# The output projection of an encoder layer as seven block products

## The chip, the cores and the metric

One core of a Trainium2 chip runs the kernel. The metric is device time in microseconds for one execution; three timed runs are shown, beside one execution taken by the hardware profiler.

## The reference

One encoder layer works on two independent groups ("prompt" and "sample") with shared weights. A group is a matrix x of 1024 tokens by 1024 channels. An input projection feeds four kinds of heads (retention, HGRN2, mLSTM, SSD); their outputs, 512 channels each, are concatenated to `mixed`, 1024 tokens by 2048 channels. What matters here is what comes after:

```python
y = jnp.einsum('bte,ed->btd', mixed, w_out)          # w_out: 2048 x 1024
x = _layer_norm(DN_ALPHA * x + y, ln_g, ln_b)
gate = jax.nn.sigmoid(jnp.einsum('btd,de->bte', x, w_ple_gate).astype(jnp.float32))
return (x + gate * jnp.einsum('btp,pd->btd', p, w_ple_proj)).astype(x.dtype)
```

`p` has 256 channels. All arrays are float32.

## The kernel before

**Numbers in two parts.** A projection operand in float32 is split in a high and a low part of the type float32r (`split`: ScalarE copies to the high part, VectorE subtracts to get the low one). A product a·b is then three matmuls: high·high, high·low, low·high. A full-width matmul has a stationary operand of 128x128 and a moving one of 128x512.

**Order of the work.** For each group 14 head units run one after another (`ORDER`); each writes its 128 channels of `mixed`, channel-major, to DRAM (`mix_d`). After both groups' units comes the tail, which the change rewrites: four blocks (group, half of the tokens). Tile pools with rotating buffers order the work: `pt` (PB = 10 buffers of 1032 columns), `rt` (RB = 7), `ht` (HB = 12 of 512 columns), weight tiles `wh`/`wl` (WB = 3 pairs of 1024 columns), staging tiles `ws` (SB = 4). Projection accumulators take the four banks of `psj`, everything else the four of `pss`. A static scheduler fixes each engine's instruction order by priority, which is program order, shifted by `late`; weight splits are moved 600 places ahead (`EARLY`). All transfers shown here go through the one queue of SyncE (SP), in that order.

**A block.** `op_half` (L1090) computes 512 output columns for 512 tokens: 16 contraction tiles, for each four token tiles of three matmuls, into the four banks. `stream` (L318) brings the weights in. The split parts of `mixed` for one block lie in 32 tiles of their own (`x_tile`, L302); during the second `op_half` of a block, `load_mix` (L315) replaces them tile by tile with those of the next block. At the end each bank is added to the scaled residual input (L160). `layer_norm` (L1111) normalises the four token tiles (the root is a power on GpSimd), transposes them on TensorE and splits them again. `gate` (L1130) makes the 1024 gated output channels of 512 tokens: per 128 channels 24 matmuls for the gate, 6 for the projection of p, then ScalarE, VectorE and the store.

**Order of the blocks.** The gate of a block is held back (`pend`) and runs between the two `op_half` of the next block, so that the layer norm has matmuls beside it. At the last block the held gate comes after the second `op_half`, then the block's own layer norm, then its own gate:

```python
op_half(g, hf, 1, ys, None if last else blocks[n + 1])
xn = parts(last)
if last and pend:
    gate(*pend)
layer_norm(ys, xn)
pend = (g, hf, xn)
```

## Time and profile before

| what | us |
|---|---|
| timed runs, median of 3 | 2713.09 |
| timed runs, lowest and highest | 2709.48, 2713.47 |
| span of the profiled execution, first to last instruction | 2708.0 |
| of that, the tail (from 2106 us on) | 602.0 |

The profiled execution has no separate timing beside its span; the median of the timed runs stands 5.1 us above it. Engines are named PE (TensorE matmuls), PEld (weight loads into TensorE), DVE (VectorE), ACT (ScalarE), POOL (GpSimd) and SP (SyncE, here the issuer of DMAs). L174 is the line of the kernel that issues every split matmul, L148 and L151 are ScalarE's copy and VectorE's two-input operation, whoever calls them. `po` are the banks of the output projection, `pg` and `pq` those of the gate, `ptl` those of the transposes. A matmul's own duration overlaps its neighbours'; pace is read from starts in the chain of waits.

### The profile page before, as it was taken

The numbers are of one execution on the slowest core, as the hardware profiler recorded it, in microseconds if no ns is written. First come the engines' busy times: TensorE is split into PE (matmuls) and PEld (weight loads), VectorE is DVE, ScalarE is ACT, GpSimd is POOL, SyncE is SP. The second block draws the span as 40 slices with busy tenths as digits, with TensorE's granted clock in tenths as the row PEclk, the third lists the DMA queues.
The fourth block names the chain that finished last, engine by engine and source line by source line (L and its number), as shares of the span: only waits on it lengthen the run. The fifth ranks groups of instructions, "written<-read, shape, count | busy, mean of one in ns | idle before, by whom it ended". The sixth has DMA issues, their size and how long they took to land.

```text
span 2708.0 us, 43819 instructions
## 1 busy us (share of the span) xinstructions
PE 2665.3 (98%) x16874; PEld 2384.2 (88%) x16874; DVE 1806.3 (67%) x4417; ACT 1095.3 (40%) x2197; POOL 55.6 (2%) x48
## 2 busy tenths in 40 slices
PE   9999999999999999999999999999999999999999
PEld 8889988879899999999898888989999888888887
DVE  7778768878755555787786878855455555546455
ACT  6656523444422313655533444432222343333323
POOL 0000000000000000000000000000000000000000
PEclk9999999999999999999999999999999999999999
DMA  4111011334321213111111241432122434535333
GB/s 148 47 41 39 24 51 41 94 94 94 86 71 48 78 40 105 44 48 35 41 38 41 75 105 51 91 105 67 56 63 89 164 121 136 190 122 195 128 113 105
DMA packets 172945, 225.15 MB, mean 83 GB/s; under 512 B 13888, under 2 KB 82112, under 8 KB 172736
## 3 DMA queue, kind: packets, MB, share of 16 engines
q1 hardware_dynamic: 172736, 222.34, 27.0%
q8 instruction: 133, 2.18, 0.3%
q14 instruction: 76, 0.62, 0.1%
HBM read 196.86 MB, written 25.43 MB: 82 GB/s over the span
## 4 chain that ended last, share of the span: by engine, by line
PE 93%; DVE 3%; DMA 2%; ACT 1%; issue 1%; POOL 0%; SPq 0%; DVEq 0%; ACTq 0%; POOLq 0%
PE pj L174 53%; PE po L174 13%; PE pg L174 7%; PE pov L177 5%; PE psc L177 5%; PE pst L177 4%; PE ptr L399 3%; PE pin L177 2%; PE pq L174 2%; DMA ub<-ud 1%; DMA ub<-fd 1%; DVE x L160 0%; DMA ws<-in_wp 0%; PE ptl L1125 0%; ACT wh L148 0%
## 5 line engine op out<-in xcount | busy, mean ns | idle before, releaser
L174 PE MATMUL pj<-wl,xh 128*128 128x256 f32 (+1 forms) x2304 | 664.2, 288 | 0.0
L174 PE MATMUL pj<-wh,xh 128*128 128x256 f32 (+1 forms) x2304 | 663.6, 288 | 0.3
L174 PE MATMUL pj<-wh,xl 128*128 128x256 f32 (+1 forms) x2304 | 662.7, 288 | 0.0
L151 DVE TENSOR_TENSOR wl<-ws,wh 128x512 fp32r<-128x512 f32 (+1 forms) x488 | 313.8, 679 | 303.0 <-ACT wh L148 299.8
L148 ACT ACTIVATE wh<-ws 128x512 fp32r<-128x512 f32 (+1 forms) x488 | 280.7, 617 | 468.3 <-PE pj L174 234.4
L174 PEld LDWEIGHTS pj<-wh,xh 128*128 128x128 f32 x2304 | 441.4, 192 | 2.6 <-DVE hB L154 1.1
L174 PEld LDWEIGHTS pj<-wl,xh 128*128 128x128 f32 x2304 | 441.6, 192 | 1.4
L174 PEld LDWEIGHTS pj<-wh,xl 128*128 128x128 f32 x2304 | 441.6, 192 | 0.6
L174 PE MATMUL pj<-xh,wh 128*128 128x512 f32 x1024 | 415.9, 406 | 5.8 <-ACT wh L148 5.8
L174 PE MATMUL pj<-xh,wl 128*128 128x512 f32 x1024 | 414.7, 405 | 0.0
L174 PE MATMUL pj<-xl,wh 128*128 128x512 f32 x1024 | 413.3, 404 | 0.0
L174 PEld LDWEIGHTS pj<-xh,wh 128*128 128x128 f32 x1024 | 194.2, 190 | 40.6 <-ACT wh L148 5.8
L174 PEld LDWEIGHTS pj<-xl,wh 128*128 128x128 f32 x1024 | 194.3, 190 | 34.7
L174 PEld LDWEIGHTS pj<-xh,wl 128*128 128x128 f32 x1024 | 194.1, 190 | 34.7 <-DVE wl L151 0.2
L174 PE MATMUL po<-wl,xh 128*128 128x512 f32 x512 | 202.9, 396 | 0.0
L174 PE MATMUL po<-wh,xh 128*128 128x512 f32 x512 | 202.1, 395 | 0.0
L174 PE MATMUL po<-wh,xl 128*128 128x512 f32 x512 | 202.1, 395 | 0.0
L174 PE MATMUL pg<-xn,wh 128*128 128x512 f32 x384 | 120.2, 394 | 0.0
L174 PEld LDWEIGHTS po<-wl,xh 128*128 128x128 f32 x512 | 96.2, 188 | 21.0
L174 PEld LDWEIGHTS po<-wh,xl 128*128 128x128 f32 x512 | 96.2, 188 | 20.4
L174 PEld LDWEIGHTS po<-wh,xh 128*128 128x128 f32 x512 | 96.2, 188 | 20.0 <-DVE g L157 0.2
L151 DVE TENSOR_TENSOR xl<-xr,xh 128x512 fp32r<-128x512 f32 x96 | 63.9, 690 | 68.5 <-ACT xh L148 66.5
(285 smaller groups left out, 4262.6 us busy)
## 6 DMA issues: line engine op xcount, KB each, us to landing
ws<-in_wp SPq DMA_DIRECT2D x472, 256.0 KB, 3.3
mix<-hZ SPq DMA_DIRECT2D x64, 256.0 KB, 2.8
ub<-fd SPq DMA_DIRECT2D x64, 256.0 KB, 7.3
ub<-ud SPq DMA_DIRECT2D x64, 256.0 KB, 7.1
xr<-mix SPq DMA_DIRECT2D x64, 256.0 KB, 5.1
xr<-in_xT SPq DMA_DIRECT2D x32, 256.0 KB, 5.1
xr<-in_x SPq DMA_DIRECT2D x32, 256.0 KB, 5.0
out<-sg SPq DMA_DIRECT2D x32, 256.0 KB, 2.0
```

Of the source, the lines that this page charges most:

```text
L148: S.activation(o, i, AF.Copy, scale=scale)
L151: V.tensor_tensor(o, a, b, op)
L174: TE.matmul(o, l, r, start=start, stop=stop)
L177: TE.matmul(o, l, r, start=start, stop=stop)
L399: TE.transpose(o[0:s.shape[1], P * n:P * n + s.shape[0]], s, ident[0:s.shape[0], 0:s.shape[0]])
```

## The change

The tail no longer works by halves of the tokens. For a group, `mixed` (tokens in 2 halves, channels in 2 halves) times `w_out` (channels in 2 halves, columns in 2 halves) is a product of 2x2 blocks, and is computed with seven block products instead of eight, in Winograd's form of Strassen's method. Each product has 512 tokens, 1024 channels (8 contraction tiles) and 512 columns, and takes the four `psj` banks. `PROD` lists them in order with their operands: `("p", ...)` is a block as it is, `("c", ...)` a sum that is kept in a running tile (`RUN`), `("s", ...)` a sum used once. Four products need sums of blocks of `mixed`, and four sums of blocks of `w_out`; both kinds work on 128x512 tiles, the first on GpSimd, the second on VectorE (`fetch`). `join` puts a finished product into the output blocks, adding the residual when a block is to be complete. `prep_x` prepares the operands of the product after next (or, at m = 5, of the next group's first), into the two sets of 16 tiles that the halves had before. The first half of the tokens is normalised after the product numbered 3, and transposed between the matmuls of the last two products. Then come both gates of the group; the second half is transposed between the matmuls of the first gate. The pools grow: PB 10 to 12, RB 7 to 8, SB 4 to 5; the scratch for dynamic DMAs is set to 1024 bytes.

The diff, without the comments and docstrings that it also removes:

```diff
-PB, RB, HB, WB, SB, SSB = 10, 7, 12, 3, 4, 3
+PB, RB, HB, WB, SB, SSB = 12, 8, 12, 3, 5, 3
+SCRATCH = 1024
 SLACK = [0, 0]
 EARLY = 600
-L = [160, 500, 80, 100, 180, 80, 180]
...
-        def load_mix(g, hf, n):
-            x_tile(n // NKT, n % NKT, mix_d[g][n, :, 512 * hf:512 * hf + 512])
-
...
-        # ======================= output projection, layer norm, per-layer input gate =======================
-        def op_half(g, hf, n, ys, nxt=None):
-            """512 columns of the residual sum of 512 tokens."""
+        ADD, SUB = ALU.add, ALU.subtract
+        X11, X12, X21, X22 = [("p", i, j) for i in range(2) for j in range(2)]
+        RUN = ("k",)
+        PROD = [
+            (1, X11, X11),
+            (2, X12, X21),
+            (5, ("c", X21, X22, ADD), ("c", X12, X11, SUB)),
+            (6, ("c", RUN, X11, SUB), ("c", X22, RUN, SUB)),
+            (3, ("s", X12, RUN, SUB), X22),
+            (7, ("s", X11, X21, SUB), ("s", X22, X12, SUB)),
+            (4, X22, ("s", RUN, X21, SUB)),
+        ]
+        KH = DI // P // 2
+        run = {}
+        def mix_at(g, a, k):
+            return mix_d[g][KH * a[2] + k, :, 512 * a[1]:512 * a[1] + 512]
+        def out_at(b, k):
+            off, n, kt = PIECE_AT[("out", b[2])]
+            src = wp[off:off + P * kt * n].rearrange("(p f) -> p f", p=P)
+            r = KH * b[1] + k
+            return src[:, r * n:r * n + n]
+        def fetch(new, at, spec, k, key):
+            add = nc.gpsimd.tensor_tensor if key[0] == "x" else tt
+            def get(a, o=None):
+                if a == RUN:
+                    return run[key][k]
+                o = new() if o is None else o
+                nc.sync.dma_start(o, at(a, k))
+                return o
+            if spec[0] == "p":
+                return get(spec)
+            if spec[0] == "c" and RUN not in spec:
+                o = run[key][k]
+                get(spec[1], o)
+                add(o, o, get(spec[2]), spec[3])
+                return o
+            two = [get(a) for a in spec[1:3]]
+            o = run[key][k] if spec[0] == "c" else two[spec[1] == RUN]
+            add(o, two[0], two[1], spec[3])
+            return o
+        def running(key):
+            two = [pt("run") for _ in range(KH // 2)]
+            run[key] = [two[k // 2][:, 512 * (k % 2):512 * (k % 2) + 512] for k in range(KH)]
+        xq = {}
+        def prep_x(g, m, slot, k):
+            spec = PROD[m][1]
+            if k == 0 and spec[0] == "c" and RUN not in spec:
+                running(("x", g))
+            r = fetch(lambda: ht("xr"), lambda a, n: mix_at(g, a, n), spec, k, ("x", g))
+            h = xp.tile([P, 512], F32R, tag=f"xh{slot}{k}", name=nm("xh"))
+            l = xp.tile([P, 512], F32R, tag=f"xl{slot}{k}", name=nm("xl"))
+            split(h, l, r)
+            xq[g, m, k] = h, l
+        def out_stream(g, m):
+            spec = PROD[m][2]
+            if spec[0] == "c" and RUN not in spec:
+                running(("w", g))
+            for k in range(0, KH, 2):
+                h = wq.tile([P, 1024], F32R, tag="wh", name=nm("wh"))
+                l = wq.tile([P, 1024], F32R, tag="wl", name=nm("wl"))
+                for r in range(2):
+                    o = slice(512 * r, 512 * r + 512)
+                    with late(-EARLY):
+                        s = fetch(lambda: st.tile([P, 512], F32, tag="ws", name=nm("ws")), out_at, spec, k + r, ("w", g))
+                        split(h[:, o], l[:, o], s)
+                for r in range(2):
+                    yield h[:, 512 * r:512 * r + 512], l[:, 512 * r:512 * r + 512]
+        def product(g, m, Y, nxt):
             acc = [psj.tile([P, 512], F32, tag="pj", name=nm("po")) for _ in range(4)]
-            cols = slice(512 * n, 512 * n + 512)
-            k = 0
-            for wh, wl in stream(("out", n)):
-                xk = xh[divmod(k, NKT)], xl[divmod(k, NKT)]
+            pairs = out_stream(g, m)
+            w = {}
+            def step(k, t):
+                tk = slice(P * t, P * t + P)
+                (xh_, xl_), (wh, wl) = xq[g, m, k], w[k]
+                mm(acc[t], xh_[:, tk], wh, k == 0, False)
+                mm(acc[t], xh_[:, tk], wl, False, False)
+                mm(acc[t], xl_[:, tk], wh, False, k == KH - 1)
+            for k in range(KH - 2):
+                w[k] = next(pairs)
                 for t in range(4):
-                    tk = slice(P * t, P * t + P)
-                    mm(acc[t], xk[0][:, tk], wh, k == 0, False)
-                    mm(acc[t], xk[0][:, tk], wl, False, False)
-                    mm(acc[t], xk[1][:, tk], wh, False, k == DI // P - 1)
+                    step(k, t)
                 if nxt:
-                    load_mix(*nxt, k)
-                k += 1
+                    nxt(k)
+            w[KH - 2], w[KH - 1] = next(pairs), next(pairs)
             for t in range(4):
+                step(KH - 2, t)
+                step(KH - 1, t)
+                join(g, PROD[m][0], t, acc[t], Y)
+            if nxt:
+                nxt(KH - 2)
+                nxt(KH - 1)
+        def join(g, p, t, acc, Y):
+            a, b = slice(0, 512), slice(512, 1024)
+            y0, y1 = Y[0][t], Y[1][t]
+            def plus_x(y, hf, cols):
                 xr = ht("xr")
                 r0 = 512 * hf + P * t
                 nc.sync.dma_start(xr, x[g, r0:r0 + P, cols])
-                stt(ys[t][:, cols], xr, ALPHA, acc[t], ALU.mult, ALU.add)
-        def layer_norm(ys, dst):
-            """Normalised tokens, channel-major, in two float32r parts."""
+                stt(y[:, cols], xr, ALPHA, y[:, cols], ALU.mult, ALU.add)
+            if p == 1:
+                copy(y0[:, b], acc)
+            elif p == 2:
+                tt(y0[:, a], acc, y0[:, b], ADD)
+                plus_x(y0, 0, a)
+            elif p == 5:
+                copy(y1[:, b], acc)
+            elif p == 6:
+                tt(y1[:, a], acc, y0[:, b], ADD)
+                tt(y0[:, b], y1[:, a], y1[:, b], ADD)
+                plus_x(y0, 0, b)
+                plus_x(y1, 1, b)
+            elif p == 3:
+                tt(y0[:, b], y0[:, b], acc, ADD)
+            elif p == 7:
+                tt(y1[:, a], y1[:, a], acc, ADD)
+                tt(y1[:, b], y1[:, b], y1[:, a], ADD)
+                plus_x(y1, 1, a)
+            else:
+                tt(y1[:, a], y1[:, a], acc, SUB)
+        def normalise(ys):
             for t in range(4):
                 y = ys[t][:, 0:D]
                 bst, agg = small(12, "lb"), small(2, "la")
...
                 V.bn_aggr(agg, bst)
                 r = rstd_of(agg[:, 1:2], 1, "lr")
                 ts(y, y, agg[:, 0:1], ALU.subtract, r, ALU.mult)
-            for c in range(NKT):
-                tr = ps("ptl")
-                with late(L[6]):
-                    for t in range(4):
-                        TE.transpose(tr[:, P * t:P * t + P], ys[t][:, P * c:P * c + P], ident)
-                m = ht("lm")
-                act(m, tr, AF.Identity, bias=par[:, C_LNB + c:C_LNB + c + 1], scale=par[:, C_LNG + c:C_LNG + c + 1])
-                split(dst[0][c], dst[1][c], m)
-        def gate(g, hf, xn):
+        def turn(ys, dst, c):
+            tr = ps("ptl")
+            for t in range(4):
+                TE.transpose(tr[:, P * t:P * t + P], ys[t][:, P * c:P * c + P], ident)
+            m = ht("lm")
+            act(m, tr, AF.Identity, bias=par[:, C_LNB + c:C_LNB + c + 1], scale=par[:, C_LNG + c:C_LNG + c + 1])
+            split(dst[0][c], dst[1][c], m)
+        def gate(g, hf, xn, then=None):
             tok = slice(512 * hf, 512 * hf + 512)
             ph, pl = pt("ph", F32R), pt("pl", F32R)
             for k in range(PLE // P):
...
                     stt(s, s, 1.0, pq, ALU.add, ALU.mult)
                     stt(s, s, 0.5, xf, ALU.mult, ALU.add)
                     nc.sync.dma_start(out[g, P * ct:P * ct + P, tok], s)
+                    if then:
+                        then(ct)
         def next_x(i):
             for k in range(2 * NKT):
                 if i + 1 < len(groups):
                     load_x(groups[i + 1], k)
                 elif tail:
-                    load_mix(groups[0], 0, k)
+                    prep_x(groups[0], k // KH, k // KH, k % KH)
         for i, g in enumerate(groups):
             for j, (b, n) in enumerate(order):
...
                     todo[b](g, n, done)
         if not tail:
             return
-        blocks = [(g, hf) for g in groups for hf in range(2)]
-        def parts(last):
-            if last:
-                h = [xp.tile([P, 512], F32R, tag=f"xh0{k}", name=nm("nh")) for k in range(NKT)]
-                l = [xp.tile([P, 512], F32R, tag=f"xl0{k}", name=nm("nl")) for k in range(NKT)]
-                return h, l
-            both = []
-            for _ in range(2):
-                two = [pt("xn", F32R) for _ in range(4)]
-                both.append([two[k // 2][:, 512 * (k % 2):512 * (k % 2) + 512] for k in range(NKT)])
-            return both
-        pend = None
-        for n, (g, hf) in enumerate(blocks):
-            ys = [rt("y") for _ in range(4)]
-            op_half(g, hf, 0, ys)
-            last = n == len(blocks) - 1
-            if pend and not last:
-                gate(*pend)
-            op_half(g, hf, 1, ys, None if last else blocks[n + 1])
-            xn = parts(last)
-            if last and pend:
-                gate(*pend)
-            layer_norm(ys, xn)
-            pend = (g, hf, xn)
-        gate(*pend)
+        seq = [(g, m) for g in groups for m in range(len(PROD))]
+        def bring(n):
+            return (lambda k: prep_x(*seq[n], n % 2, k)) if n < len(seq) else None
+        n = 0
+        for g in groups:
+            Y = [[rt("y") for _ in range(4)] for _ in range(2)]
+            two = [pt("xn", F32R) for _ in range(8)]
+            half = [two[k // 2][:, 512 * (k % 2):512 * (k % 2) + 512] for k in range(2 * NKT)]
+            xa = half[0:NKT], half[NKT:]
+            slot = (n + len(PROD) - 1) % 2
+            xb = []
+            def between(m, ahead):
+                def f(k):
+                    if ahead:
+                        ahead(k)
+                    c = KH * (m - len(PROD) + 2) - KH // 2 + k
+                    if 0 <= c < NKT:
+                        turn(Y[0], xa, c)
+                return f
+            def then(ct):
+                for c in range(2 * ct - 2, 2 * ct):
+                    if 0 <= c < NKT:
+                        turn(Y[1], xb, c)
+            for m in range(len(PROD)):
+                product(g, m, Y, between(m, None if m == len(PROD) - 1 else bring(n + 2)))
+                n += 1
+                if PROD[m][0] == 3:
+                    normalise(Y[0])
+            xb += [[xp.tile([P, 512], F32R, tag=f"x{c}{slot}{k}", name=nm("n" + c)) for k in range(NKT)] for c in "hl"]
+            normalise(Y[1])
+            gate(g, 0, xa, then)
+            gate(g, 1, xb)
+            rest = bring(n + 1)
+            for k in range(KH):
+                if rest:
+                    rest(k)
...
-    nc = bacc.Bacc("TRN2", target_bir_lowering=False, num_devices=1)
+    nc = bacc.Bacc("TRN2", target_bir_lowering=False, num_devices=1, dynamic_dma_scratch_size=SCRATCH)
```

## Rows read from the trace of the kernel before

**Rows 1.** The page's head and its part 1: engines over the whole span.

```profile
span 2708.0 us, 43819 instructions
...
PE 2665.3 (98%) x16874; PEld 2384.2 (88%) x16874; DVE 1806.3 (67%) x4417; ACT 1095.3 (40%) x2197; POOL 55.6 (2%) x48
```

**Rows 2.** Windows before and after 2106 us: length, busy time by engine.

```profile
0.00:2106.00 2106.00, 2069.58 (x14173) 1896.69 (x14174) 1484.71 (x3865) 880.52 (x1828) 44.93 (x31) 0.99 0.23 66
2106.00:2708.00 602.00, 595.73 (x2703) 487.52 (x2702) 321.56 (x553) 214.77 (x370) 10.72 (x17) 1.00 0.43 142
```

**Rows 3.** Chain of waits, 2300 to 2410 us: start, length, what.

```profile
2305.62 65.28 PE po L174 x288
2370.91 0.22 PE ptl L1125 x2
...
2384.94 11.58 PE po L174 x51
2396.52 5.56 PE pg L174 x24
...
2403.46 5.56 PE pg L174 x24
```

**Rows 4.** Chain of waits, 2630 to 2708 us.

```profile
2633.81 1.38 PE pq L174 x6
2635.20 5.35 PE pg L174 x23
2640.55 0.02 issue
...
2648.20 5.76 PE pg L174 x24
```

**Rows 5.** Timeline of VectorE at the end of a round: start, length, what.

```profile
2347.51 2.47 DVE L160 SCALAR_TENSOR_TENSOR y<-xr,po 128x512 f32<-128x512 f32 x4
```

**Rows 6.** Groups of instructions, 2106 to 2708 us: count, busy us, mean ns.

```profile
L151 DVE TENSOR_TENSOR wl<-ws,wh 128x512 fp32r<-128x512 f32 x206 | 133.7, 687 | 131.9 <-ACT wh L148 131.9
...
L148 ACT ACTIVATE wh<-ws 128x512 fp32r<-128x512 f32 x204 | 118.5, 623 | 208.5 <-PE po L174 121.9 <-PE pg L174 73.8 <-DMA ws<-in_wp 7.3
...
L145 ACT ACTIVATE lm<-ptl,par 128x512 f32<-128x512 f32 x32 | 24.3, 777 | 7.3 <-PE ptl L1125 7.2
...
L1117 DVE BATCH_NORM_STATS2 lb<-y 128x6 f32<-128x512 f32 x32 | 21.2, 675 | 0.0
...
L157 DVE TENSOR_SCALAR y<-y,la,lr 128x1024 f32<-128x1024 f32 x16 | 13.0, 812 | 4.2 <-POOL lr L406 3.3
...
L1118 DVE BATCH_NORM_AGGREGATE la<-lb 128x2 f32<-128x12 f32 x16 | 3.0, 201 | 0.0
...
L157 DVE TENSOR_SCALAR lra<-la 128x1 f32<-128x1 f32 x16 | 2.3, 143 | 0.1
```

**Rows 7.** Waits of SP's DMA queue, 2106 to 2708 us: total, times, longest.

```profile
SPq L330 <- DVE wl L151: 316.2, 186, 11.4
```

**Rows 8.** DMA view, 2106 to 2708 us: GB/s in 40 equal slices, issues.

```profile
GB/s 106 70 170 336 205 126 78 98 166 99 122 123 137 243 321 122 102 106 175 71 122 137 143 294 284 104 105 72 250 121 83 105 85 147 131 153 81 134 94 52
...
xr<-mix SPq DMA_DIRECT2D x48, 256.0 KB, 4.9
```

**Rows 9.** Groups of instructions on GpSimd by shape, whole span.

```profile
L406 POOL TENSOR_TENSOR rs<-rsa,nhalf 128x8 f32<-128x8 f32 x28 | 46.4, 1656 | 2082.7 <-DVE rsa L157 2082.7
L406 POOL TENSOR_TENSOR lr<-lra,nhalf 128x1 f32<-128x1 f32 x16 | 9.1, 568 | 458.9 <-DVE lra L157 456.0 <-DVE la L1118 2.9
```

**Rows 10.** Timeline, 2594.7 to 2597.5 us.

```profile
2594.78 0.64 DVE L160 SCALAR_TENSOR_TENSOR sg<-sg,xf 128x512 f32<-128x512 f32 x1
2594.89 0.93 POOL L406 TENSOR_TENSOR lr<-lra,nhalf 128x1 f32<-128x1 f32 x1 [2.92 <-DVE la L1118]
...
2596.87 0.55 POOL L406 TENSOR_TENSOR lr<-lra,nhalf 128x1 f32<-128x1 f32 x1 [1.06 <-DVE lra L157]
```

More of the change, by code (lines that the diff above doesn't have):

```diff
@@ L32 @@
 BLK = 8
-PB, RB, HB, WB, SB, SSB = 10, 7, 12, 3, 4, 3
+PB, RB, HB, WB, SB, SSB = 12, 8, 12, 3, 5, 3
+SCRATCH = 1024
 SLACK = [0, 0]
 EARLY = 600
-L = [160, 500, 80, 100, 180, 80, 180]
+L = [160, 500, 80, 100, 180, 80]
 ORDER = [("hg", 0), ("hg", 1), ("hg", 2), ("hg", 3), ("ret", 0), ("ssd", 0), ("ml", 0), ("ssd", 1),
```

## The prediction

> **What bounds the kernel now.** I read the table of engines first [rows 1]: TensorE is busy 98% of the span, VectorE 67%, ScalarE 40%, GpSimd 2%. A busy share of 98% can still hide slow spots, so I then cut the span in two at 2106 us, where the output projection's matmuls begin [rows 2]. In the stage that the change rewrites, 602 us long, TensorE is idle 6.3 us, VectorE works 322 us (53%) and GpSimd 10.7 us. The chain of waits says the same more strictly [rows 3]: 288 projection matmuls follow each other in 65.28 us, 226.7 ns each; then come 14.0 us in which transposes and projection matmuls alternate, 51 more matmuls, and the gate at once. From 2305.62 to 2396.52 are 90.9 us; 384 matmuls at 226.7 ns take 87.05 us, so the 32 transposes cost 0.12 us each and nothing is left over as idle. Only near the end does the chain leave TensorE: between the last two gates it runs through ScalarE from 2640.55 to 2648.20 [rows 4]. So in this stage time is matmul count times 226.7 ns, as long as VectorE keeps up.
>
> **Removed.** Before: 8 calls of op_half, 16 contraction tiles x 4 token tiles x 3 matmuls = 192 each, 1536 in all. After: 2 groups x 7 products x 8 x 4 x 3 = 1344. The matmuls have the same shape and operands of the same type. 192 x 226.7 ns = 43.5 us less on the path. Gates (960 matmuls) and transposes (128) stay. One product takes 96 x 226.7 ns = 21.76 us; I call this a period.
>
> **Moved: the last layer norm.** Before, the last block is normalised and transposed with no matmuls beside it: 7.65 us, of which 6 gate matmuls (1.4 us) and 32 transposes (3.85 us) are work that stays [rows 3, 4]. In the change both gates of a group follow its last product, and the second half's transposes sit between the matmuls of the first gate. 2.4 us of idle go. The cover is the first gate, 8 x 6.94 = 55.5 us [rows 3]; VectorE's own gate work and one normalisation fit under it.
>
> **Added on VectorE.** A 128x512 operation is listed at 0.68 us, but four in a row take 2.47 us, 0.60 us each [rows 5, 6]; I use 0.605. Per period there are 8 weight splits, mostly 8 splits of the mixed channels for the product after next, 8 weight sums in four of the seven products, and the join of the finished product. Operations per period, in the order of the list PROD: 16, 24, 24, 40, 20, 36, 16+4. In us: 9.7, 14.5, 14.5, 24.2, 12.1, 21.8, 12.1. The sixth period also holds the first half's normalisation, 4 x (2 x 0.675 + 0.201 + 0.143 + 0.812) = 10.0 us by single durations [rows 6], and 4 splits of transposed tiles, 2.4 us; the seventh the other 4. In all about 124 us against 7 x 21.76 + 32 x 0.12 = 156 us of TensorE: 79%. The mean fits. Two periods do not: the fourth is over by 24.2 - 21.8 = 2.4 us, the sixth by 34.2 - 23.7 = 10.5 us. What isn't ready earlier is exposed: at most 12.9 us a group, 25.8 us in all; at least nothing, since weights run ahead (the DMA queue waited 316 us for a weight buffer to come free [rows 7], so loads were early) and operands of the mixed channels are prepared one product ahead. I take a third, 9 us, because the period before the sixth is light (12.1 of 21.8 us) but the normalisation can't begin before that period's join.
>
> **The joins and the four banks.** A product uses all four projection banks and the next needs them back. Before, the four evacuations of one round (2.47 us from 2347.51) ran while the next round's matmuls already followed at 226.7 ns [rows 5, 3]: cost nothing. The change has the token tiles end 1.36 us apart (6 matmuls), so most joins have more room than that; the one with four operations a tile (2.4 us) is the burst counted above. Nothing more is added.
>
> **ScalarE.** 16 splits a period at 0.623 us [rows 6] are 10.0 us of 21.76; two joins that copy add 4 x 0.6. Hidden. The transposed tiles' scaling (777 ns [rows 6]) is 8 a group more in the crowded half than before, 6 us over two periods; hidden too.
>
> **DMA.** Loads of mixed channels rise from 64 to 144 tiles, of output weights from 128 to 144, 256 KB each: 25.2 MB more. A group loads 72 + 72 + 16 tiles, 41.9 MB in 152 us, 276 GB/s; slices of the stage before have reached 336 GB/s [rows 8]. The fourth period asks for 32 tiles, 385 GB/s, and spills some 3 us into the light fifth. All go through SP's queue in order, and each weight load there waits for a buffer, now with five instead of four behind it. I put it at nothing; bare, the spill is 3 us a group.
>
> **GpSimd adds.** 4 x 8 sums a group, 64 in all, none in the trace. From below: VectorE's subtraction of the same shape, 0.687 us [rows 6]. From above: GpSimd's power takes 0.568 us for 1 column and 1.656 us for 8 [rows 9], 0.155 us a column, 80 us for 512. A sum is nearer to VectorE's row than to a power; with GpSimd's floor of 0.57 us on top I take 1.26 us. Eight are 10.1 us of a period: hidden, since the sums of a product are made two products ahead. The four products that need them are prepared from the first period on and the last is used in the sixth, so 32 sums have 5 x 21.76 = 109 us and up to 3.4 us each is free. The Trainium skill (GPSIMD Engine Reference, section Elementwise — side-by-side cycle accounting) gives 4497 ns for an add of 2048 columns, a quarter of which, 1.12 us, is an estimate for 512; the sum would not change by it, and no row here shows it.
>
> **Do the sums hold up VectorE?** GpSimd waits for VectorE in one place that can be seen: the power that usually takes 0.55 us took 0.93 us when a VectorE operation with two SBUF inputs had begun 0.11 us before it [rows 10]. The reverse isn't shown, as those powers read one column. From below nothing; from above every sum stops VectorE for its 1.26 us: 40 us a group on top of the 62.9 us of the first four periods, 103 against 87 us. I keep it as a rival, at zero in the sum. The Trainium skill (SBUF — State Buffer, section Who interferes with whom) says that a VectorE instruction with two SBUF inputs and a GpSimd instruction that reads SBUF exclude each other, whichever starts second waiting for the other's end. The trace agrees for the one direction, 0.93 against 0.55 us; by the rule splits, weight sums and half of the joins would be held as well, which is the second rival's time.
>
> **Pool sizes.** Larger pools also let the first 2106 us be ordered anew. TensorE is idle 36 us there [rows 2], the most that could be gained; I see no row that blames these pools, and take zero.
>
> **Sum.** -43.5 - 2.4 + 9 = -37 us. The profiled span of 2708.0 becomes 2671; the median of the timed runs stands 5.1 us above that span, so 2713.1 becomes 2676.
>
> **Rivals.**
> 1. TensorE stays the bound, as summed: 2662 to 2686. For it: 79% VectorE load, no idle before. Chance 0.60.
> 2. VectorE and GpSimd hold each other up. Per group 16 us in the first four periods and 12.9 from the bursts, less 9.7 us of slack in the fifth: 19 us, 38 in all if nothing is absorbed, so -46 + 38 = -8, 2705; half of it absorbed, 2686. For it: the 0.93 us row. Against: operands are ready a product ahead. Chance 0.22 for 2686 to 2706, with 0.04 of that within no change.
> 3. Slower: a sum costs far more than VectorE's. From 4.0 us a sum (3.4 free, then 64 us lost for each further us against 37 gained) the kernel is slower; at 6 us, 64 x 2.6 - 37 = +129, 2842. For it: 0.155 us a column of a power. Against: an add is no power. Chance 0.07.
> 4. The first 2106 us are reordered by the pools: some 20 us better, 2656 (0.06), or as much worse than the sum and the bursts at their bound (0.05, around no change: 0.03 within it, 0.02 beyond).
>
> **Numbers.** Predicted 2676. The range 2659 to 2702 holds the first, most of the second and part of the fourth. A measurement of this kernel can tell about 0.2%, 5 us. Faster by more: 0.60 + 0.18 + 0.06 = 0.84; within: 0.04 + 0.03 = 0.07; slower: 0.07 + 0.02 = 0.09.
>
> **What would show it.** 1344 projection matmuls at 226.7 ns, and a stage some 565 us long with TensorE idle under 16 us: the count and the bursts are right. VectorE's subtractions well over 0.69 us while GpSimd adds run, in the first four products of a group only: rival 2. GpSimd sums over 3.4 us and TensorE waiting on ScalarE splits behind them: rival 3. A start of the stage far from 2106 us: rival 4. What would make me wrong is a wait at each product's start for weights or a bank, which the old stage never showed.

## The result: 0.6% slower, and the profile after

The changed kernel takes 2725.4 us (median of 4 runs, 2722.0 to 2732.6), the kernel before 2711.3 beside it: ratio 1.0062, 95% interval 1.0042 to 1.0082. (Ratios here are those on record; the quotient of two medians can differ from them by about 0.001.) The prediction was 2676 us with a range of 2659 to 2702; the time lies outside it, on the other side of no change.

The page's head and table of engines after, to be read beside [rows 1]:

```profile
span 2722.4 us, 43912 instructions
...
PE 2634.3 (97%) x16682; PEld 2353.0 (86%) x16682; DVE 1948.9 (72%) x4569; ACT 1121.8 (41%) x2245; POOL 166.5 (6%) x112
```

192 matmuls are gone, and TensorE is still named busy 97% of the span. The stage is what tells. The same windows as in [rows 2] (length, busy time of PE, PEld, VectorE, ScalarE and GpSimd, granted clock, DMA share, GB/s), cut where the projection's first matmul stands now:

```profile
0.00:2103.00 2103.00, 2066.49 (x14170) 1893.62 (x14171) 1485.16 (x3864) 880.57 (x1827) 45.44 (x31) 1.00 0.23 67
2103.00:2722.00 619.00, 567.83 (x2514) 459.33 (x2512) 463.72 (x706) 241.19 (x419) 121.02 (x81) 0.97 0.53 176
```

The stage was to take 565 us; it takes 619, against 602 before. TensorE works 28 us less in it and idles 51 us instead of 6.3. VectorE works 464 us instead of 322, GpSimd 121 instead of 11.

From the starts of matmuls on the timeline, one product of 96 matmuls lasts, in the order of `PROD`, in us (from the start of the last matmul of the product before, in a group's first product from its own first; 21.8 is the pace of [rows 3], 23.7 with the transposes that lie in the last two):

| product | 1 | 2 | 5 | 6 | 3 | 7 | 4 |
|---|---|---|---|---|---|---|---|
| first group | 30.3 | 23.0 | 44.6 | 22.8 | 24.6 | 27.6 | 26.2 |
| second group | 21.6 | 30.3 | 31.4 | 22.2 | 30.2 | 24.5 | 26.2 |

They sum to 385.5 us; 14 x 21.76 and 64 transposes of 0.12 us are 312. So 73 us are lost. The kernel before loses 9 us of this kind, all in its first two stretches of 96 matmuls (29.8 and 22.8 us). So 64 us are new, against 43.5 + 2.4 us removed and 2.7 us by which the stage starts earlier: +15 worked out, +14.4 between the two profiled spans. Of the 73 us, TensorE's waits of more than 0.15 us make 47, of which 37 end with a join on VectorE, and matmuls at half the clock (below) some 11.

The worst product, 44.6 us, shows what is lost. TensorE's timeline after (start, length, instruction, idle time before it and what ended it):

```profile
2156.63 0.39 PE L175 MATMUL po<-wh,xl 128*128 128x512 f32 x1
2169.37 0.77 PE L175 MATMUL po<-wh,xh 128*128 128x512 f32 x1 [12.35 <-DVE y L152]
2169.93 0.63 PE L175 MATMUL po<-wl,xh 128*128 128x512 f32 x1
...
2175.05 0.55 PE L175 MATMUL po<-wl,xh 128*128 128x512 f32 x1
2175.43 0.39 PE L175 MATMUL po<-wh,xl 128*128 128x512 f32 x1
...
2181.92 0.79 PE L175 MATMUL po<-wh,xh 128*128 128x512 f32 x1 [5.41 <-DVE y L152]
```

What TensorE waits for is `y`: VectorE has not yet taken the second product out of its bank. For this first matmul of the third product the operands are there; what is missing is a join. VectorE's timeline of the same stretch says why the join is late:

```profile
2154.46 1.70 DVE L152 TENSOR_TENSOR xl<-run,xh 128x512 fp32r<-128x512 f32 x1 [4.81 <-ACT xh L149]
...
2159.46 3.42 DVE L152 TENSOR_TENSOR wl<-run,wh 128x512 fp32r<-128x512 f32 x2
2162.80 3.42 DVE L152 TENSOR_TENSOR run<-ws,run 128x512 f32<-128x512 f32 x2
2166.14 2.48 DVE L152 TENSOR_TENSOR xl<-run,xh 128x512 fp32r<-128x512 f32 x4
2168.55 0.68 DVE L152 TENSOR_TENSOR y<-po,y 128x512 f32<-128x512 f32 x1
...
2174.33 6.33 DVE L152 TENSOR_TENSOR xl<-run,xh 128x512 fp32r<-128x512 f32 x5
...
2181.19 1.28 DVE L152 TENSOR_TENSOR y<-po,y 128x512 f32<-128x512 f32 x2
```

Two things are to be seen. The bank was full soon after 2156.63, and the first `y<-po,y` stands behind splits and sums for later products, the second 12.6 us behind the first. The four `xl<-run,xh` at 2166.14 are still operands of the third product, the five at 2174.33 belong to the fourth. And `wl<-run,wh` and `run<-ws,run`, two SBUF inputs each, start 1.67 us apart instead of 0.60, while `xl<-run,xh` at 2166.14, in a gap between GpSimd's sums, keep 0.60. The `y<-po,y` shown, with one input in PSUM, start while no GpSimd sum runs and say nothing on that; of the stage's 16, five ran beside a sum, and they took 676 to 683 ns like the others. GpSimd's timeline has the other half:

```profile
2152.47 1.29 POOL L1134 TENSOR_TENSOR run<-run,xr 128x512 f32<-128x512 f32 x1 [7.83 <-DMA xr<-mix]
2154.32 9.67 POOL L1134 TENSOR_TENSOR run<-run,xr 128x512 f32<-128x512 f32 x6 [0.56 <-DMA xr<-mix]
2163.96 1.71 POOL L1138 TENSOR_TENSOR run<-run,xr 128x512 f32<-128x512 f32 x1
2169.72 1.84 POOL L1138 TENSOR_TENSOR run<-run,xr 128x512 f32<-128x512 f32 x1 [4.06 <-DMA xr<-mix]
2172.19 6.72 POOL L1138 TENSOR_TENSOR run<-run,xr 128x512 f32<-128x512 f32 x4 [0.63 <-DVE wl L152]
```

A sum while VectorE is idle takes 1.29 us; six in a row beside VectorE 1.61 each. Both engines move at one pace of 1.6 to 1.7 us, one operation of each per beat.

The sums also come late. GpSimd stood 7.83 us for a load of the mixed channels, and until 2154.46 VectorE stood 4.81 us for ScalarE's copy of that sum. The chain of waits that leads to these joins goes back to such a load, which SP's queue issued behind eight weight loads (2139.57 to 2147.60):

```profile
2148.12 5.74 DMA xr<-mix
```

The stage's groups of instructions (count, busy us, mean ns, idle time before) say it in the mean; [rows 6] has 687 ns for such a subtraction:

```profile
L152 DVE TENSOR_TENSOR wl<-run,wh 128x512 fp32r<-128x512 f32 x32 | 34.7, 1124 | 0.0
L152 DVE TENSOR_TENSOR xl<-run,xh 128x512 fp32r<-128x512 f32 x32 | 34.7, 1117 | 11.3 <-ACT xh L149 10.9
...
L1138 POOL TENSOR_TENSOR xr<-xr,xr 128x512 f32<-128x512 f32 x16 | 29.8, 1883 | 28.2 <-DMA xr<-mix 16.7 <-DVE wl L152 8.1 <-DVE y L161 3.2
...
L1134 POOL TENSOR_TENSOR run<-run,xr 128x512 f32<-128x512 f32 x16 | 25.5, 1617 | 149.8 <-DMA ws<-in_wp 123.6 <-DMA xr<-mix 26.1
...
L152 DVE TENSOR_TENSOR y<-po,y 128x512 f32<-128x512 f32 x16 | 10.4, 680 | 0.0
```

One more loss comes on top. Windows of 10 us within that product (columns as above):

```profile
2165.00:2175.00 10.00, 5.63 (x13) 4.46 (x14) 10.00 (x12) 2.93 (x5) 5.32 (x4) 0.50 0.74 234
...
2190.00:2200.00 10.00, 10.00 (x46) 8.28 (x45) 10.00 (x8) 5.97 (x11) 7.93 (x5) 1.00 0.29 88
```

Having idled 12.35 us, TensorE is granted half the clock, 0.50: the matmuls from 2169.93 to 2175.05 start 0.427 us apart, twice the 0.227 of full speed, so at 1.2 instead of 2.4 GHz. The 14 steps from 2169.37 to 2175.43 take 6.06 us instead of 3.17, and the nine after the second wait, from 2181.92 on, 3.87 instead of 2.04. That accounts for this product: 17.8 us of two waits and 4.7 of low clock, of 22.8 lost. Over the whole stage 50 steps fall in stretches granted 0.50; at 0.2 us and a little more each they make the 11 us above.

### The profile page after: what moved, and what is told of

Same layout as the page of the kernel before. It is cut to its first block, busy times and chain, and to the rows that moved or that the text cites. A ratio compares the mean times of both kernels' runs of the same rounds, so it can differ in the third digit from the quotient of the medians.

```text
span 2722.4 us, 43912 instructions
## 1 busy us (share of the span) xinstructions
PE 2634.3 (97%) x16682; PEld 2353.0 (86%) x16682; DVE 1948.9 (72%) x4569; ACT 1121.8 (41%) x2245; POOL 166.5 (6%) x112
## 3 DMA queue, kind: packets, MB, share of 16 engines
q1 hardware_dynamic: 186560, 247.52, 29.8%
## 4 chain that ended last, share of the span: by engine, by line
PE 84%; DVE 7%; DMA 5%; issue 2%; POOL 1%; ACT 1%; SPq 0%; DVEq 0%; POOLq 0%; ACTq 0%
PE pj L175 53%; PE pg L175 6%; PE psc L178 5%; PE pov L178 5%; PE po L175 4%; PE pst L178 4%; PE ptr L397 3%; PE pin L178 2%; DMA ws<-in_wp 2%; PE pq L175 2%; DMA xr<-mix 2%; DVE wl L152 2%; DVE xl L152 1%; DMA ub<-ud 1%; DVE x L161 1%
## 5 line engine op out<-in xcount | busy, mean ns | idle before, releaser
L152 DVE TENSOR_TENSOR wl<-ws,wh 128x512 fp32r<-128x512 f32 (+1 forms) x440 | 286.6, 688 | 224.9 <-ACT wh L149 218.1
L149 ACT ACTIVATE wh<-ws 128x512 fp32r<-128x512 f32 (+1 forms) x440 | 252.2, 616 | 378.4 <-PE pj L175 243.9
L175 PE MATMUL po<-wh,xh 128*128 128x512 f32 x448 | 182.8, 408 | 43.7 <-DVE y L152 37.2
L175 PE MATMUL po<-wl,xh 128*128 128x512 f32 x448 | 179.5, 401 | 0.1
L175 PE MATMUL po<-wh,xl 128*128 128x512 f32 x448 | 177.9, 399 | 0.0
L404 POOL TENSOR_TENSOR rs<-rsa,nhalf 128x8 f32<-128x8 f32 x28 | 46.9, 1674 | 2079.4 <-DVE rsa L158 2079.4
L175 PEld LDWEIGHTS po<-wh,xh 128*128 128x128 f32 x448 | 86.7, 194 | 68.8 <-DVE y L152 22.4
L149 ACT ACTIVATE xh<-xr 128x512 fp32r<-128x512 f32 x112 | 68.2, 629 | 99.8 <-PE po L175 52.4
L178 PE MATMUL psc<-a,k 128*128 128x128 f32 x768 | 104.0, 278 | 0.0
L175 PEld LDWEIGHTS po<-wh,xl 128*128 128x128 f32 x448 | 86.7, 193 | 18.7
```

Of the source, the lines that this page charges most:

```text
L149: S.activation(o, i, AF.Copy, scale=scale)
L152: V.tensor_tensor(o, a, b, op)
L175: TE.matmul(o, l, r, start=start, stop=stop)
L178: TE.matmul(o, l, r, start=start, stop=stop)
L404: nc.gpsimd.tensor_tensor(q, r, nhalf[:, 0:n], ALU.pow)
```

## Experiments

Four causes stand against each other: GpSimd's sums and VectorE's operations hold each other up (the collision); the joins, and with them the banks, come late in VectorE's order (late joins); the sums are too much work or too many loads, wherever they are made (work); the larger pools. In the expectations the first is theory A, the second D, the third B or F for work and C for loads. All ratios are to the kernel before.

**1. Sums on VectorE.**

```diff
-            add = nc.gpsimd.tensor_tensor if key[0] == "x" else tt
+            add = tt
```

> The changed kernel with the 64 sums of the mixed channels on VectorE instead of GpSimd. Theory A (the shared port: a GpSimd sum and a VectorE operation with two SBUF inputs exclude each other, and banks come free late because the joins queue behind the held operations): VectorE has 39 us more work of its own (64 x 0.605), but no operation over 0.7 us; the longest product falls from 44.6 us to under 30, and the time to 2685-2705. Theory B (VectorE is simply overloaded, whoever holds it): the added work makes it worse, 2730-2760. Theory C (loads with too few buffers behind one queue): no change from the port, 2715-2735, with the chain on transfers as before.

Measured: 2710.8 us, ratio 1.0008 (0.9996 to 1.0019), 14.6 us better than the change and outside all three ranges. Every two-input operation is back at 0.68 to 0.69 us. But the third product still takes 40.2 us. The window over it, then VectorE's and TensorE's timeline in it:

```profile
2158.00:2199.00 41.00, 24.60 (x101) 19.83 (x100) 40.77 (x68) 17.75 (x31) 0.00 (x0) 0.79 0.73 246
```

```profile
2172.16 1.88 DVE L152 TENSOR_TENSOR xl<-run,xh 128x512 fp32r<-128x512 f32 x3
2173.96 0.68 DVE L152 TENSOR_TENSOR run<-run,xr 128x512 f32<-128x512 f32 x1
2174.56 1.28 DVE L152 TENSOR_TENSOR y<-po,y 128x512 f32<-128x512 f32 x2
```

```profile
2175.39 0.77 PE L175 MATMUL po<-wh,xh 128*128 128x512 f32 x1 [16.40 <-ACT xh L149]
```

Sums on GpSimd are a cause and aren't all: with no GpSimd in the way VectorE is still full, and the join again stands behind a long run of preparation for later products. The profile puts TensorE's wait down to a copy of ScalarE that ended at 2175.30; that copy is for the fourth product, and the first join ended at 2175.24, so I read it as the join's. Runs 6 and 7 test that.

**2. No sums of the mixed channels** (a plain block instead, and its one load).

```diff
-            spec = PROD[m][1]
+            spec = next(a for a in (PROD[m][1], *PROD[m][1][1:3]) if a[0] == "p")
```

> The changed kernel with a plain block in place of every sum of mixed channels: leaves out the 64 sums and 32 of their second loads, so the output is not the reference's. It is the floor without GpSimd's share. Theory A: 2670-2690, all VectorE operations at 0.60-0.69 us. Theory B: 2690-2710, since VectorE keeps the same operations of its own. Theory C: 2680-2700, gained by the loads left out.

Measured: 2690.0 us, ratio 0.9940 (0.9924 to 0.9957). The third product falls to 31.8 us. These 64 sums with 32 of their loads cost 35 us as the change makes them; it doesn't say by which of the causes, and 2690 is the edge of two ranges and within the third.

**3 and 4. The kernel before, with 64 GpSimd additions, or with 64 GpSimd writes, in `load_mix`.** The two say whether it is GpSimd's work or its reading of SBUF.

```diff
         def load_mix(g, hf, n):
-            x_tile(n // NKT, n % NKT, mix_d[g][n, :, 512 * hf:512 * hf + 512])
+            r = x_tile(n // NKT, n % NKT, mix_d[g][n, :, 512 * hf:512 * hf + 512])
+            nc.gpsimd.tensor_tensor(extra[1], r, extra[0], ALU.add)   # run 3
+            nc.gpsimd.memset(r, 0.0)                                  # run 4
...
```

Left out of the diff: `x_tile` returns its tile, `extra` are two tiles of their own, the first set to zero, and the scratch is that of the change.

> The kernel before with 64 GpSimd additions of 128x512 put beside its VectorE work in the tail (each reads a tile of mixed channels that is being split; the result is unused). Theory A: GpSimd's addition takes 1.1-1.3 us alone and up to 1.9 beside VectorE, VectorE's splits there go from 0.69 to 1.1 us or more, and the time hardly moves (2710-2722), since VectorE is only half busy there. Theory B or C: splits stay at 0.69 us, time unchanged.

> The kernel before with 64 GpSimd operations of 128x512 in the places of e3's additions, but which only write (a tile that has been split is set to zero). Theory A in the form of a shared read port: VectorE's splits stay at 0.69 us and the time at that of before, 2705-2712. If any GpSimd operation on SBUF holds VectorE up: splits at 0.8 us or more, as in e3 (0.81 and 1.13), and 2712-2720.

Measured: with additions 2716.6 us, 1.0040 (1.0025 to 1.0055); with writes 2707.9 us, 1.0002 (0.9993 to 1.0011). Groups of the stage, with additions, then with writes:

```profile
L151 DVE TENSOR_TENSOR wl<-ws,wh 128x512 fp32r<-128x512 f32 x206 | 158.4, 806 | 128.8 <-ACT wh L148 128.7
L321 POOL TENSOR_TENSOR extra<-xr,extra 128x512 f32<-128x512 f32 x51 | 80.5, 1579 | 222.4 <-DMA xr<-mix 218.9
L151 DVE TENSOR_TENSOR xl<-xr,xh 128x512 fp32r<-128x512 f32 x54 | 59.8, 1126 | 16.0 <-ACT xh L148 16.0
```

```profile
L151 DVE TENSOR_TENSOR wl<-ws,wh 128x512 fp32r<-128x512 f32 x204 | 132.5, 687 | 131.0 <-ACT wh L148 130.8
L151 DVE TENSOR_TENSOR xl<-xr,xh 128x512 fp32r<-128x512 f32 x53 | 36.4, 692 | 55.2 <-ACT xh L148 55.2
L321 POOL MEMSET xr<- 128x512 f32 x53 | 27.9, 526 | 331.5 <-DVE xl L151 309.0 <-issue 13.5 <-DMA ws<-in_wp 4.4
```

No result of these additions is used, and yet `xl` has a mean of 1126 ns: on the timeline 1609 for the 29 that ran beside an addition, 685 for the 28 that did not. With as many operations that only write, nothing moves. Here `xl` is a weak witness, since a write waits for the `xl` of its own tile (309.0 us of GpSimd's idle time in its row) and few run beside one; but 40 of the `wl` ran beside a write, and they took 685 ns. So it is reading that collides. In the kernel before it costs 8 us by the medians and 11 by the ratio, and only the first round of 96 matmuls is longer (38.7 us instead of 29.8); the others keep their time.

**5. The kernel before, with the larger pools.**

```diff
-PB, RB, HB, WB, SB, SSB = 10, 7, 12, 3, 4, 3
+PB, RB, HB, WB, SB, SSB = 12, 8, 12, 3, 5, 3
...
```

The smaller scratch goes with it.

> The kernel before with the larger pools of the change alone (12, 8 and 5 buffers, smaller scratch). The changed kernel reached its tail at 2103.4 us against 2106.1 us: all theories expect 2705-2712, within 0.2% of before. A gain or loss of more than 6 us would mean that the pools carry part of the result.

Measured: 2708.1 us, 1.0002 (0.9993 to 1.0012). The pools fall out.

**6 and 7. The joins moved ahead, with the sums on VectorE (and so with the line of run 1) or on GpSimd.**

```diff
-                join(g, PROD[m][0], t, acc[t], Y)
+                with late(-EARLY):
+                    join(g, PROD[m][0], t, acc[t], Y)
```

The whole of `join` moves, so the loads and additions of the residual too.

> Sums of the mixed channels on VectorE, and the joins moved 600 places ahead in the scheduler's order, as the weight splits are. Theory D (what is left after the port is out of the way is order: joins queue behind operands that are needed only later, so banks come free late): the third product falls from 40.2 and 32.6 us to under 28, time 2685-2700. Theory F (what is left is the amount of work: VectorE is full for a product and a half): 2705-2715, the same products long.

> The changed kernel, sums on GpSimd, with the joins alone moved 600 places ahead. Theory A (the port: held operations) with D: the waits for banks go, the slow operations stay: 2700-2715. Theory A alone, with operands late rather than banks: 2720-2728. Theory F: 2720-2728.

| | joins in program order | joins 600 places ahead |
|---|---|---|
| sums on GpSimd | 2725.4 | 2719.3, ratio 1.0035 (1.0023 to 1.0047) |
| sums on VectorE | 2710.8 | 2689.8, ratio 0.9931 (0.9916 to 0.9946) |

One line gives 21.0 us once the sums are off GpSimd, and 6.1 with them there; sums on GpSimd cost 29.5 us with early joins, 14.6 with late ones. By the length of the stage alone it is 20.6 and 10.6, 26.4 and 16.3, as both versions with early joins begin it at 2109 us, 4 to 6 us later than the other two. With sums on VectorE the third product falls from 40.2 to 22.5 us, as theory D had it. The loads of the sums are the same in this run, so late loads cost that product time by way of the joins that stand behind them. On GpSimd it falls from 44.6 to 30.7, but the fourth rises from 22.8 to 35.0, and 2719.3 us lies between the ranges. TensorE's waits in the stage, after the change and then with early joins and sums on VectorE (total, times, longest; a weight load's wait, PEld, overlaps that of its matmul):

```profile
PE po L175 <- DVE y L152: 37.2, 10, 12.3
...
PEld po L175 <- DVE y L152: 22.4, 9, 6.7
```

```profile
PEld po L175 <- DVE y L152: 13.6, 12, 3.2
...
PE po L175 <- DVE y L152: 8.7, 8, 2.8
```

What is left with early joins and sums on GpSimd isn't the collision alone. Timelines of TensorE, ScalarE and GpSimd before its fourth product:

```profile
2201.11 0.79 PE L175 MATMUL po<-wh,xh 128*128 128x512 f32 x1 [7.53 <-ACT y L149]
2197.05 0.63 ACT L149 ACTIVATE xh<-xr 128x512 fp32r<-128x512 f32 x1 [8.26 <-POOL xr L1138]
2195.40 11.22 POOL L1138 TENSOR_TENSOR xr<-xr,run 128x512 f32<-128x512 f32 x7 [7.28 <-DMA xr<-mix]
```

The bank waits for a join's copy that ScalarE makes in its order behind copies of sums, and the sum waits for its load. So the 14.6 and 29.5 us are the price of the sums on GpSimd, the collision and this chain together; no run here separates the two.

**8. No sums at all** (plain blocks everywhere): the floor.

```diff
+            spec = next(a for a in (PROD[m][1], *PROD[m][1][1:3]) if a[0] == "p")
...
+            spec = next(a for a in (PROD[m][2], *PROD[m][2][1:3]) if a[0] == "p")
```

> A plain block in place of every sum, of mixed channels and of weights: leaves out all 128 sums and the 64 second loads, so the output is not the reference's. It is the floor of this structure: 1344 matmuls and joins, no sums. Sum of the prediction without bursts: 2713 - 46 = 2667. Theory F: 2665-2675. Theory D: 2675-2690, since joins and operands stay in the same order.

Measured: 2671.8 us, 0.9865 (0.9851 to 0.9880). The seven products, joins and gates by themselves are worth about what the matmul count says. What the sums still cost in run 6, as work and loads, is 2689.8 - 2671.8 = 18.0 us.

**9 and 10. Sums made ahead of the stage.** All sums made once by VectorE beside earlier matmuls, in four buffers of their own, kept in DRAM, and loaded as plain tiles; those of the weights once for both groups. In 9 the weights' sums go with the first group's units; in 10 they follow the first group's mixed sums among the second group's units, and all of the second group's mixed sums stand in the first gate.

```diff
-            (5, ("c", X21, X22, ADD), ("c", X12, X11, SUB)),
...
+            (5, ("q", 0), ("q", 0)),
...
+                if i == 0 and 2 <= j < 10:
+                    presum(("w", 0), out_at, j - 2)          # run 9; in run 10 behind presum_x(0, j - 1)
+                if i == 1 and 1 <= j < 9:
+                    presum_x(0, j - 1)
...
```

> All sums, of mixed channels and of weights, made on VectorE outside the products: the weights' 32 once, among the first group's head units, the first group's 32 among the second group's units, the second group's there and in the first gate; they are stored and loaded back as plain operands. 96 sums instead of 128, 96 x 4 more transfers in all. Pool of 10 large buffers instead of 12, as the running tiles go. Theory F: product stage close to the matmul pace, 2668-2685 if the head units absorb 58 us of VectorE work at no more than 5 us. Theory D: joins still queue behind operands, 2685-2700. If the head units can't absorb it, the tail starts late, past 2112 us.

> As e7_sums_ahead, but the weights' sums stand behind the first group's sums of mixed channels, so that they can't be drawn into the first 200 us (where e7's TensorE lost 7 us), and all the second group's sums lie in the first gate. Theory F: the tail stays about 562 us long, as in e7; the head loses under 15 us instead of 36, time 2670-2690. If head units can't absorb the sums wherever they lie, 2695-2710.

Measured: 2706.8 us, 0.9992 (0.9982 to 1.0002), and 2687.0 us, 0.9926 (0.9910 to 0.9943). In both the stage takes 562 to 563 us, the joins in program order, with products at 21.6 to 23.7 us but for the first of the stage and the last of each group. Windows of the second:

```profile
0.00:2116.00 2116.00, 2069.64 (x14169) 1895.82 (x14170) 1531.96 (x3940) 879.42 (x1827) 45.95 (x31) 0.99 0.29 85
2116.00:2679.00 563.00, 553.28 (x2515) 453.08 (x2514) 385.36 (x662) 241.17 (x419) 10.62 (x17) 1.00 0.56 185
```

The first version loses 36 us before the stage, 7 of them in the first 200 us, where the scheduler moved the weights' sums and their loads (162 GB/s instead of 78). The second starts the stage 10 us later than the kernel before. This is the fastest kernel of the study that computes the reference, level with 6.

**11. Ahead for the second group only:** the first group as in 6, its weights' sums kept for the second, whose mixed sums are made in the first gate, in `ht` buffers.

```diff
+                if g == groups[0]:
+                    presum_x(groups[1], ct)
```

> As e5_vector_joins_early for the first group, whose weight sums are kept in DRAM; the second group's products load all their sums (those of its mixed channels are made in the first gate). The head is as in e5. Theory F: the second group's products fall from 141.6 us together to about 137, the gate bears 19 us more of VectorE work, time 2680-2690. Theory D alone: 2690, no gain over e5.

Measured: 2717.1 us, 1.0037 (1.0024 to 1.0050). A miss. The last six products take 135.0 us together (141.6 in run 6, 164.8 after the change), as expected, but the first group's two gates take 150 us instead of 121 in run 6 and 114 after the change. Waits from 2240 to 2400 us:

```profile
DVE pre L152 <- DMA pre<-mix: 20.7, 7, 6.0
...
PEld pg L175 <- ACT wh L149: 12.3, 1, 12.3
```

The sums' loads share SP's queue and the 12 `ht` buffers with the gate, and the gate's weights come late. Run 10 makes the same sums in the same gate over the same queue, but in buffers of their own, and there the two gates take 114.5 us. That points to the buffers; the two runs differ in more than that.

**12. Number 10 with its 96 sums on GpSimd.** VectorE has slack before the stage; does the collision cost anything there?

```diff
-                tt(d, c, d, ADD)
+                nc.gpsimd.tensor_tensor(d, c, d, ADD)
...
```

> As e9_sums_ahead_late (2687 against 2708), with the same 96 sums on GpSimd. Theory A with F (the port costs only where VectorE has no slack): sums of 1.3 to 1.9 us, VectorE operations beside them up to 1.7 us, but the products stay at 22-23 us, since no sum lies in them; time within 6 us of e9, 2681-2693. If the port's price doesn't depend on slack: 96 sums that each hold VectorE for 1.1 us in place of 0.6 us of its own work, 2700-2720.

Measured: 2748.5 us, 1.0150 (1.0133 to 1.0167), 61 us worse than with VectorE's sums, and outside both ranges. Of the 68 us between the two profiled spans 55 lie before the stage. Between 1000 and 1400 us TensorE works 365 us of 400 (with VectorE's sums 395). Waits there, with GpSimd's sums, then with VectorE's:

```profile
DVE hX L155 <- POOL rs L405: 22.3, 5, 15.3
PEld ptr L398 <- DVE hY L155: 18.6, 3, 14.6
```

```profile
DVE hX L155 <- POOL rs L405: 9.1, 5, 1.8
...
PEld ptr L398 <- DVE hY L155: 5.3, 3, 1.8
```

Beside the collision (a product `a<-a,q` of 128x512 there takes 738 ns instead of 681) the roots of the head norms, which GpSimd computes in order, queue behind sums that wait for their loads (71 us of waits for loads of mixed channels there, the longest 29). So the run doesn't say what the collision costs where VectorE has slack. It says that GpSimd had work of its own on the path.

## Why the prediction was wrong, step by step

**Removed: right.** 1344 projection matmuls at 226.7 ns. Run 8, which has this and not the sums, takes 2672 us; the prediction's sum without its bursts is 2713 - 43.5 - 2.4 = 2667. In its profile the stage takes 561.5 us, where 602 - 43.5 - 2.4 = 556 was due, and begins at 2113.8 us.

**Moved, the last layer norm: right.** Between the last two gates the chain of waits after has only matmuls in it, where [rows 4] went through ScalarE:

```profile
2655.97 5.55 PE pg L175 x24
2661.52 1.39 PE pq L175 x6
2662.91 5.44 PE pg L175 x24
```

The last two gates with their 32 transposes take 113.7 us from first to last matmul instead of 116.6.

**"Do the sums hold up VectorE?", at zero in the sum: the first step that failed.** The bound from above was there, and the one row that bore on it [rows 10]. I took zero since operands are ready a product ahead. In the product that lost most they weren't: its last four were split at 2166.14 to 2168.55, 9 to 12 us after the product before had ended. Nor would it be cover: VectorE's time is lost whatever it works on, and in the crowded stretch the next thing in its order is a join. In full alternation each VectorE operation costs 1.07 us more (1.67 - 0.60). In the kernel's time, sums on GpSimd cost 14.6 us as the change stands, 29.5 us with the joins ahead; that holds the collision and the late sums, and the collision's share is open. By itself, beside the additions in the kernel before, it cost 8 to 11 us (run 3). The Trainium skill (SBUF — State Buffer, section Who interferes with whom) states that VectorE with two SBUF inputs contends with a GpSimd instruction that reads SBUF, and not with one that only writes it. The traces agree in both halves: 1609 ns for `xl` beside additions, 685 for `wl` beside writes. They also show the form: where both sides had a backlog, they took turns.

**"The joins and the four banks: nothing more is added": the second step that failed.** I reasoned from the room between token tiles, 1.36 us a join, as if VectorE were free when a bank is full. Before, at 53% busy, it was [rows 2, 5]. After the change its fixed order holds, between the end of a product and its join, the splits for the product after next and sums and splits of weights moved 600 places ahead; the first join came 12 us late, the second 13 after it. This is 21 us once the sums are off GpSimd (2710.8 to 2689.8), 6 with them there: where the two meet each hides part of the other. The prediction had named the sign, a wait for a bank at a product's start, and given it no price. It had put the crowding in the fourth and sixth products; the third lost most.

**Bursts, 9 us: not isolated.** With the sums off GpSimd and joins early, the sums' own work and loads cost 2689.8 - 2671.8 = 18 us, but there VectorE also makes the 64 mixed sums, 39 us of work that the term didn't hold. The term's bounds were 0 to 25.8; no row supported a third of it rather than all.

**GpSimd adds: priced at 1.26 us, measured 1.29 alone,** and 1.6 to 1.9 beside VectorE, under the 3.4 us that were free. Rival 3 did not occur: TensorE waited for joins. ScalarE did wait 81 us for GpSimd's sums; TensorE waited 1.5 us for a copy of the mixed channels. What "hidden" left out is that the sums stood 71 us for their loads, and that joins stand in order behind them.

**DMA and ScalarE: put at nothing, and nothing by themselves.** With the same loads the third product takes 22.5 us in run 6. In the change a load that comes late holds sums and ScalarE's copies, and the joins stand in order behind them.

**Not in the sum at all: the clock.** Before, the stage ran at a granted clock of 1.00; after, at 0.97, low after long waits: 4.7 us in the worst product, some 11 in the stage.

**Pools: zero, right** (run 5). **Rival 4** did not occur in the changed kernel: the stage starts at 2103.4 us.

Rival 2 had part of the mechanism, but its price had a ceiling of 38 us, all of it from VectorE's overload, and so ended at 2705: it lacked the join behind the preparation, the late sums and the clock. Taken in the order of runs 1, 6 and 8, 14.6 and 21.0 us for the two steps and 18.0 for the sums themselves make the 53.6 us from the change to run 8. What stays open: the collision's share of the sums on GpSimd, and why the stage starts anywhere from 2102.6 to 2113.8 us in versions that leave the earlier code alone.

## What to carry to other kernels

When work is added beside a saturated TensorE, list what VectorE's in-order queue holds between a full bank and the evacuation that frees it, and put the evacuation first; a mean load of 79% says nothing on that. GpSimd was no free helper for elementwise sums while VectorE had two-input work in SBUF: the two took turns, what stood behind the sums in order came late, and here the sums were cheaper on VectorE itself. Seven products instead of eight did pay, 0.7%, once sums and joins were placed by the queue that they wait in.

## What the runs showed of the hardware

- A GpSimd addition of 128x512 floats takes 1.29 us alone. In backlog with VectorE's two-input operations (0.60 us alone) each side completes one per 1.6 to 1.7 us, so VectorE drops to a little over a third of its rate; operations with one input in PSUM keep 0.68 us listed (five `y<-po,y` beside a sum: 676 to 683 ns).
- A GpSimd write of the same tile, 0.53 us, leaves VectorE at 685 ns (40 weight splits beside a write).
- After waits of 12.35 and 5.41 us TensorE's granted clock was 0.50, 1.2 GHz: matmuls started 0.427 us apart instead of 0.227, which cost 2.9 and 1.8 us.
